# Differential attention on one Trainium2 core: the context queries' scores move into the free PSUM columns of two latent score runs

## The chip, the cores and the metric

The program runs on one core of a Trainium2 chip. Its engines work side by side, each through its own queue in order: TensorE (PE, matmuls into PSUM), VectorE (DVE), ScalarE (ACT), GpSimd (POOL), and SyncE (SP), which issues most of the DMA transfers. The metric is the device time of one execution in microseconds, as the median of several runs.

## What is computed

Two layers of a diffusion backbone over 512 latent tokens and 256 context tokens, model width 1024. Layer 0 is differential attention with 8 heads, each with two maps of head width 64; layer 1 is grouped-query attention. Layer 0 is what the change touches:

```python
k_all = jnp.concatenate([k, kc], axis=1)          # 512 latent + 256 context keys
v_all = jnp.concatenate([v, vc], axis=1)

def diff(qq, kk, vv, gate):
    o1 = sweep_attention(qq[..., 0, :], kk[..., 0, :], vv)
    o2 = sweep_attention(qq[..., 1, :], kk[..., 1, :], vv)
    o = o1 - lam.astype(o1.dtype) * o2
    o = rms_norm(o, subln_g) * (1.0 - lam_init)
    o = o.reshape(o.shape[0], o.shape[1], BRANCH_WIDTH)
    return (o * jax.nn.silu(gate)) @ w_out

y = diff(q, k_all, v_all, z)                      # latent queries read all 768 keys
yc = diff(qc, kc, vc, zc) if with_ctx_out else None   # context queries read 256 context keys
```

`sweep_attention` is a softmax over the keys for blocks of 128 queries. In between, the modulation (`adaln`) of both layers needs products of the conditioning vectors with large matrices (`ada_w`).

## The kernel before, in words

All matmuls keep about fp32 precision by splitting an operand into a high and a low fp32r part and adding three products (names with `hi`/`lo`, or `h`/`l` at the end). Weights stream in as `raw`, ScalarE casts them to `whi`, GpSimd subtracts to `wlo`.

PSUM has eight banks of 512 fp32 columns. Four are the single banks `bk` for projections, PV products and the like. Four are the two score tiles `sc`, each of two banks (`sc2()` hands them out in turn).

Layer 0's attention runs head by head. A head has four latent query tiles of 128 rows (qt 0 to 3) against 768 keys, and two context query tiles (qt 4 and 5) against the 256 context keys. For a latent tile, `unit` computes the scores of both maps: map m=0 in one score tile, m=1 in the other. As keys have width 64, the two maps use the upper and lower 64 rows of the array and are issued in pairs (`for m in (1, 0)`); three products (qh kh, qh kl, ql kh) for each half of 384 keys make 12 matmuls, chained so that nothing stands between them. For each map VectorE takes the maximum of 768 scores, ScalarE the exponential with its sum, VectorE the reciprocal; GpSimd scales map 0, and VectorE subtracts lambda times map 1 into the probabilities `pp`. Two query tiles share one `pp`, which `turn` transposes: on VectorE within blocks of 32, then by a store to DRAM (`dr`) and four gathers into `at`. `pv_steps` splits `at` into `ah` and `al` (ScalarE, VectorE) and multiplies with V.

For seven heads the context tiles have a unit of their own, `unit_ctx`: both tiles in one run of 12 matmuls of 256 columns, tile qt 4 in the first bank of each score tile and qt 5 in the second; one maximum over two groups of 256 columns per map, then exponentials, reciprocals of two columns, and a `turn` of width 128. The last head (h = 7) treats its context tiles in another way, which stays as it is in substance.

In the same stretch, `grp_mm` multiplies the modulation weights: twelve loads `araw` of 1 MB, one after the other through one tile (`bufs=1`), four matmuls of 32 output rows each. `grp_load` issues the next load when these matmuls have read the tile.

What sets the order: the whole program is recorded first, then `Plan` orders it. It prices each instruction (`price`), simulates the queues (`schedule`), with prices for DMA landing by size and for VectorE and GpSimd disturbing each other (`op.kind`), and finally shifts the priorities of single groups of instructions by random amounts that the numbers of the table `MOVES` fix. So a change of a price or of this table moves instructions on all engines, in both layers.

Of the kernel before, what the change touches and what calls it, by code (L numbers as in the profile page):

```python
# [16 lines left out]
P = 128  # L17
# [71 lines left out]
DRSPLIT = 1  # L89
DRB = 6  # L90
# [3 lines left out]
def f32(ap):  # L94
# [6 lines left out]
MOVES = (121443151, 661718012, 381041855, 51234840, 372779023, 957281565, 227970257, 105033711, 68446900, 773563299,  # L101
# [22 lines left out]
SLACK = 0  # L124


# [469 lines left out]
def tile_backbone(  # L596
# [692 lines left out]
    with pl.pool("t0") as t0:  # L1289
# [149 lines left out]
        def z_proj(h):  # L1439
# [12 lines left out]
            ws.release((h, 3))  # L1452
            szt[h] = sz
            gate_mul(h)

        def s_units(h, qts):
            res, pair = [], {}

# [922 lines left out]
```

## Time and profile before

| | us |
|---|---|
| median of 3 runs | 756.37 (755.59 to 760.27) |
| the profiled execution's own time | 757.93 |
| its span, first to last instruction | 755.8 |
| mean granted TensorE clock | 0.996 |

The profile comes from one execution. In its rows, times are in us from the start of the span, in groups the last figure of the busy column is the mean duration in ns; "idle before" is the time the engine stood still just before the group, and the name behind the arrow is what it waited for. A row of the timeline gives start, length, engine, operation, output and inputs, and a count of merged instructions. L509 is the line of a helper through which all instructions go. "MATMUL ... 64*128" is a matmul that uses 64 rows of the array, "128*32" one with 32 output rows. Matmuls overlap, so the price of one is read from start to start.

### The profile page before, as it was taken

The page shows a single profiled execution, that of the slowest core. Times are in us where ns is not written, and L with a number is a line of the kernel's source. Part 1 is how long each engine was busy: PE and PEld are TensorE (multiplying, and loading weights), DVE is VectorE, ACT ScalarE, POOL GpSimd, SP SyncE. Part 2 cuts the span into 40 slices and gives each one's busy share as a digit, 9 for nine tenths or more (in the row PEclk, how much of TensorE's full clock was granted, in tenths as well). Part 3 has the DMA queues.
Part 4 walks back from the last instruction along what each step waited for, and adds up shares of the span by engine and source line. Part 5 has one row for each costly group of instructions (what it writes and reads, how often), then busy time and mean ns, then how long its engine had stood idle before and what let it go on. Part 6 is the DMA issues. An engine that isn't in the chain of part 4 may idle for free. (4 is left out here: it accounts for less than half of the span.)

```text
span 755.8 us, 13984 instructions
## 1 busy us (share of the span) xinstructions
PE 733.9 (97%) x5046; PEld 654.3 (87%) x5046; DVE 567.1 (75%) x881; ACT 480.0 (64%) x1085; POOL 466.7 (62%) x512
## 2 busy tenths in 40 slices
PE   7999999999999999899999999999999989999996
PEld 6788888888878898797989998899999988888986
DVE  4445899988988869787889844789547787799744
ACT  6544477767676646666569853784476776678741
POOL 5463787885795738747755412467779887674201
PEclk9999999999999999999999999999999999999999
DMA  9933263647474655835666182034436785888613
GB/s 347 405 123 124 95 198 109 188 164 223 140 221 142 212 165 176 255 100 172 229 171 179 31 307 84 2 97 157 145 117 190 224 257 163 232 239 266 165 46 111
DMA packets 51444, 131.75 MB, mean 174 GB/s; under 512 B 6448, under 2 KB 27184, under 8 KB 49840
## 3 DMA queue, kind: packets, MB, share of 16 engines
q1 hardware_dynamic: 47952, 125.73, 52.7%
q10 hardware_dynamic: 3424, 5.15, 2.1%
q8 instruction: 39, 0.64, 0.4%
q14 instruction: 29, 0.24, 0.1%
HBM read 97.56 MB, written 29.10 MB: 168 GB/s over the span
## 5 line engine op out<-in xcount | busy, mean ns | idle before, releaser
L509 PE MATMUL bk<-whi,h 128*128 128x256 f32 (+1 forms) x1184 | 244.0, 298 | 2.9 <-DVE tb L509 1.8
L509 PE MATMUL bk<-h,whi 128*128 128x512 f32 (+2 forms) x832 | 222.4, 348 | 0.1
L509 POOL TENSOR_TENSOR wlo<-raw,whi 128x256 fp32r<-128x256 f32 x200 | 171.1, 879 | 56.1 <-ACT whi L509 53.7
L509 PEld LDWEIGHTS bk<-whi,h 128*128 128x128 f32 x1184 | 189.6, 189 | 13.9 <-issue 2.9
L509 PE MATMUL bk<-wlo,h 128*128 128x256 f32 (+1 forms) x592 | 172.3, 298 | 0.0
L509 PEld LDWEIGHTS bk<-h,whi 128*128 128x128 f32 x832 | 144.4, 188 | 15.6 <-issue 2.8
L509 PE MATMUL bk<-h,wlo 128*128 128x512 f32 (+2 forms) x416 | 144.0, 348 | 0.0
L509 POOL TENSOR_SCALAR pp<-pp,sm 128x768 f32<-128x768 f32 (+1 forms) x78 | 82.0, 1054 | 68.0 <-DVE sm L509 58.4
L509 PEld LDWEIGHTS bk<-wlo,h 128*128 128x128 f32 x592 | 109.8, 188 | 4.9 <-issue 1.6
L509 DVE TENSOR_REDUCE sm<-sc 128x1 f32<-128x768 f32 (+2 forms) x114 | 101.0, 893 | 14.7 <-PE sc L509 14.5
L509 DVE TENSOR_TENSOR al<-at,ah 128x512 fp32r<-128x512 f32 x103 | 98.7, 978 | 13.7 <-ACT ah L509 9.9
L509 ACT CAST whi<-raw 128x1024 fp32r<-128x1024 f32 (+1 forms) x70 | 71.5, 1023 | 27.1 <-PE bk L509 14.9
L509 PEld LDWEIGHTS bk<-h,wlo 128*128 128x128 f32 x416 | 78.3, 188 | 8.7 <-issue 2.4
L509 ACT CAST ah<-at 128x512 fp32r<-128x512 f32 x103 | 61.7, 618 | 33.3 <-PE bk L509 21.0
L509 DVE STREAM_TRANSPOSE pp<-pp 128x1536 f32<-128x1536 f32 (+1 forms) x39 | 61.4, 1577 | 5.7 <-POOL pp L509 5.6
L509 DVE SCALAR_TENSOR_TENSOR pp<-p,sm,pp 128x768 f32<-128x768 f32 (+1 forms) x46 | 55.8, 1219 | 4.4 <-POOL pp L509 2.8
L509 PE MATMUL sc<-qk,qk 64*128 64x384 f32 (+1 forms) x480 | 50.7, 341 | 0.4 <-DVE qk L509 0.4
L509 ACT ACTIVATE jk<-bk 128x128 f32<-128x128 f32 (+4 forms) x66 | 22.7, 345 | 41.8 <-PE bk L509 22.8
L509 ACT ACTIVATE pp<-sc,sm 128x768 f32<-128x768 f32 (+1 forms) x46 | 35.4, 770 | 21.5 <-DVE sm L509 20.8
L509 PEld LDWEIGHTS sc<-qk,qk 64*128 64x128 f32 x480 | 38.3, 184 | 10.7 <-issue 3.5
L509 POOL TENSOR_TENSOR sz<-sz,za 128x384 f32<-128x384 f32 (+1 forms) x24 | 28.3, 1180 | 23.8 <-ACT za L509 23.8
L509 ACT ACTIVATE za<-za 128x384 f32<-128x384 f32 (+1 forms) x72 | 40.0, 559 | 4.7 <-DVE za L509 4.1
(206 smaller groups left out, 1365.1 us busy)
## 6 DMA issues: line engine op xcount, KB each, us to landing
dr<-pp SPq DMA_DIRECT2D x32, 768.0 KB, 4.0
at<-dr SPq DMA_DIRECT2D x128, 192.0 KB, 4.3
raw<-in_a_w SPq DMA_DIRECT2D x30, 512.0 KB, 3.9
araw<-in_ada_g SPq DMA_DIRECT2D x12, 1024.0 KB, 7.0
raw<-in_b_w SPq DMA_DIRECT2D x20, 512.0 KB, 3.8
ag<-in_ada_s SPq DMA_DIRECT2D x16, 512.0 KB, 9.9
raw<-in_w_out SPq DMA_DIRECT2D x16, 512.0 KB, 4.5
sw<-qr ACTq DMA_DIRECT2D x32, 128.0 KB, 2.1
```

The source lines that it names most:

```text
L509: self.ops.append(getattr(eng, meth)(*args, **kw))
```

## The change

For heads 0 to 6 the separate context unit goes. The scores of context tile 4 are computed at the end of the run of latent tile 2, those of tile 5 at the end of the run of latent tile 3 (`CTX_AT`), into columns 768 to 1023 of the same score tiles, which the latent scores leave free. So that a matmul stays within one bank, the latent keys are cut into 512 and 256 columns instead of twice 384, in all heads. The two units then do their softmax for both the 768 and the 256 columns; reciprocals and the product with lambda work on two columns at once. The exponential of map 1 of the context rows goes into the tile (`at128`) that later takes the transposed result, where it had gone into a tile `p1`. A head's keys count as read (`s_end`) after its second pair of latent tiles. In the planner, the factor for single-input work on GpSimd goes from 0.25 to 0.6, the landing prices of transfers of 128 KB and 1 MB change, and `MOVES` is a new, shorter table.

```diff
+CTX_AT = {2: 0, 3: 1}
-MOVES = (121443151, 661718012, 381041855, 51234840, 372779023, 957281565, 227970257, 105033711, 68446900, 773563299,
...
+MOVES = (361629762, 413672696, 596582793, 497724196, 683463327, 110464215, 110999015, 165414765, 369530505, 1059228683,
...
-                op.kind = 0.75 if n <= 8 else 0.5 if sum(free_size(a) > 8 for a in ins) >= 2 else 0.25
+                op.kind = 0.75 if n <= 8 else 0.5 if sum(free_size(a) > 8 for a in ins) >= 2 else 0.6 if q == "POOL" else 0.25
...
-                rate, base = {196608: (207, 1450), 786432: (420, 900), 131072: (350, 2500)}.get(op.cost, (350, 1450))
+                rate, base = {196608: (207, 1450), 786432: (420, 900), 131072: (300, 1500), 1048576: (300, 2400)}.get(op.cost, (350, 1450))
...
-    def turn(pool, pp, w=384):
+    def turn(pool, pp, w=384, at=None):
...
-        at = pool.tile([P, 4, w], F32, tag=f"at{w}", name=nm("at"), bufs=ATB if w == 384 else 1)
+        if at is None:
+            at = pool.tile([P, 4, w], F32, tag=f"at{w}", name=nm("at"), bufs=ATB if w == 384 else 1)
...
+        def s_mm(sc, h, qt, lo, w, prev):
+            qh, ql, kh_, kl_ = qk[h]
+            tok = slice(qt * P, (qt + 1) * P)
+            for i, (a, b) in enumerate(((qh, kh_), (qh, kl_), (ql, kh_))):
+                for m in (1, 0):
+                    r = slice(m * 64, m * 64 + 64)
+                    o = flat_sc(sc[m])[:, lo:lo + w]
+                    if qt < NQ:
+                        b_ = b[r, lo:lo + w]
+                    else:
+                        o, b_ = by_a(o, 64), by_a(b[r, :], 192)[:, :, P:]
+                    with after(prev), chained(prev):
+                        prev = nc.tensor.matmul(o, a[r, tok], b_, start=i == 0, stop=i == 2)
+            return prev
...
             def unit(qt):
...
+                e = CTX_AT.get(qt) if h < KT - 1 else None
+                l = small(4)
+                sc = [sc2(), sc2()]
+                prev = s_mm(sc, h, qt, 0, 512, None)
+                prev = s_mm(sc, h, qt, 512, C, prev)
+                if e is not None:
+                    s_mm(sc, h, NQ + e, T, C, prev)
+                    if e == 0:
+                        ctx_tiles[h] = (
+                            t0.tile([P, 8, 2, 32], F32, tag="p0", name=nm("pp"), bufs=1),
+                            t0.tile([P, 4, P], F32, tag="at128", name=nm("at"), bufs=1))
+                    cp_, ct = ctx_tiles[h]
+                    cs = [unit_view(cp_, e), ct.rearrange("p a c -> p (a c)")[:, e * C:e * C + C].rearrange("p (b x) -> p b x", x=32)]
...
+                n = 1 if e is None else 2
+                for m in range(2):
+                    mx = small(2)
+                    for j in range(n):
+                        src = flat_sc(sc[m])[:, j * T:j * C + T]
+                        nc.vector.tensor_reduce(mx[:, j:j + 1], src, AX.X, ALU.max, negate=True)
+                        nc.scalar.activation(
+                            (cs if j else ps_)[m], src.rearrange("p (b x) -> p b x", x=32), AF.Exp, bias=mx[:, j:j + 1],
+                            accum_out=l[:, 2 * m + j:2 * m + j + 1])
+                    r = l[:, 2 * m:2 * m + n]
+                    nc.vector.reciprocal(r, r)
+                    if m == 1:
+                        nc.vector.tensor_tensor(r, r, nlam.to_broadcast([P, n]) if n > 1 else nlam, ALU.mult)
...
+                if qt % 2:
+                    res.append(turn(t0, pair[0]))
+                if e == 1:
+                    ctx_at[h].append(turn(t0, cp_, P, ct))
...
-            def unit_ctx():
...
-                for qt in (NQ, NQ + 1):
...
-                    nc.vector.tensor_reduce(mx, sc[m][:, :, :C], AX.X, ALU.max, negate=True)
...
-                if ch == 2:
+                if ch == (1 if h < KT - 1 else 2):
                     wrap(u[-1], None, lambda h=h: s_end(h))
```

How this moves instructions, at three places. First TensorE, at a context tile's scores. `sc_74` and `sc_75` are the two score tiles, the `qk` names are a head's qh, ql, kh, kl, and `h`/`whi` are activations and weights of a projection. Before, in head 1, the run of the context unit starts behind a projection's matmul:

```order
L509 MATMUL bk_70<-h_535,whi_1199 128x256
L509 MATMUL sc_75<-qk_1178,qk_1176 128x256
L509 MATMUL sc_74<-qk_1178,qk_1176 128x256
L509 MATMUL sc_75<-qk_1179,qk_1176 128x256
L509 MATMUL sc_74<-qk_1179,qk_1176 128x256
L509 MATMUL sc_75<-qk_1178,qk_1177 128x256
L509 MATMUL sc_74<-qk_1178,qk_1177 128x256
```

After, in head 3, the same forms follow the 512 columns of a latent tile:

```order
L501 MATMUL sc_75<-qk_2104,qk_2103 128x512
L501 MATMUL sc_74<-qk_2104,qk_2103 128x512
L501 MATMUL sc_75<-qk_2104,qk_2102 128x256
L501 MATMUL sc_74<-qk_2104,qk_2102 128x256
L501 MATMUL sc_75<-qk_2105,qk_2102 128x256
L501 MATMUL sc_74<-qk_2105,qk_2102 128x256
L501 MATMUL sc_75<-qk_2104,qk_2103 128x256
L501 MATMUL sc_74<-qk_2104,qk_2103 128x256
```

The six rows of 256 columns stand there twice in a row, first for the last latent keys, then for the context tile; then a projection goes on. In all, 41 score runs become 34, of which 14 have 18 matmuls.

Second, SP's queue around two loads of `araw` in head 3's stretch; `dr` is the store of transposed probabilities, `at` the gathers. Before:

```order
L509 DMA dr_2691<-pp_2600 128x1536
L509 DMA araw_2556<-in_ada_g 128x2048
L509 DMA at_2690<-dr_2691 32x4x384 x4
L509 DMA raw_2647<-in_a_w 128x1024
L509 DMA dr_2743<-pp_2726 128x512
L509 DMA araw_2702<-in_ada_g 128x2048
```

After:

```order
L501 DMA raw_2643<-in_a_w 128x1024
L501 DMA araw_2538<-in_ada_g 128x2048
L501 DMA araw_2725<-in_ada_g 128x2048
L501 DMA dr_2699<-pp_2590 128x1536
L501 DMA raw_2810<-in_a_w 128x1024
L501 DMA dr_2706<-pp_2588 128x512
```

The store and gathers that stood around and between the two loads now stand behind both. On TensorE the groups of matmuls that read these loads have 35 ordinary matmuls between them before, 38 wider ones and a score run after.

Third, TensorE in layer 1, where a query projection (`whi`, `wlo` with the tokens `h`) ends in a bank and the next one begins. Before:

```order
L509 MATMUL bk_72<-whi_7209,h_730_5258 128x256
L509 MATMUL bk_72<-wlo_7210,h_730_5258 128x256
L509 MATMUL bk_72<-whi_7209,h_731_5259 128x256
L509 MATMUL bk_72<-whi_7200,h_730_5258 128x256
L509 MATMUL bk_72<-wlo_7201,h_730_5258 128x256
L509 MATMUL bk_72<-whi_7200,h_731_5259 128x256
```

After, at the same projection:

```order
L501 MATMUL bk_71<-whi_7167,h_695_5216 128x256
L501 MATMUL bk_71<-wlo_7168,h_695_5216 128x256
L501 MATMUL bk_71<-whi_7167,h_696_5217 128x256
L501 MATMUL bk_73<-al_7516,vh 128x256 x2
L501 MATMUL bk_73<-ah_7568,vh 128x256 x2
L501 MATMUL bk_73<-ah_7568,vl 128x256 x2
L501 MATMUL bk_73<-al_7569,vh 128x256 x2
L501 MATMUL bk_73<-ident,q_6675 128x128
L501 MATMUL bk_73<-ident,q_6729 128x128
L501 MATMUL bk_73<-ident,q_6790 128x128
L501 MATMUL bk_73<-ident,q_6844 128x128
L501 MATMUL bk_71<-whi_7158,h_695_5216 128x256
```

PV products and transposes now stand between the two projections in that bank. On ScalarE, the squares for that query tile's norm (`jk`) stood behind the cast `qh` of the transposed query tile. Before:

```order
L509 CAST ah_7557<-at_7451 128x512
L509 CAST ah_7610<-at_7451 128x512
L509 COPY g_1125_7555<-bk_73 128x4x2x32
L509 CAST qh_7750<-bk_73 128x512
L509 ACTIVATE jk_7713,sm_7712<-bk_72 128x128
L509 ACTIVATE jk_7715,sm_7712<-bk_72 128x128
```

After:

```order
L501 CAST ah_7568<-at_7409 128x512
L501 CAST ac_7925<-gacc 128x512
L501 ACTIVATE jk_7671,sm_7670<-bk_71 128x128
L501 ACTIVATE jk_7673,sm_7670<-bk_71 128x128
L501 COPY g_1090_7513<-bk_73 128x4x2x32
L501 ACTIVATE sm_7720<-sm_7718,qrs_6672 128x1
```

They now stand ahead of the copy of the PV result (`g`), and the cast of the query tile comes some rows later.

More of the change, by code (lines that the diff above doesn't have):

```diff
@@ new lines, in unit @@
+                if qt % 2 == 0:
+                    pair[0] = t0.tile([P, 24, 2, 32], F32, tag="pp", name=nm("pp"), bufs=PPB)
+                ps_ = [unit_view(pair[0], qt % 2), t0.tile([P, T], F32, tag="p1", name=nm("p"), bufs=2).rearrange("p (b x) -> p b x", x=32)]
+                n = 1 if e is None else 2
[11 more added lines that the diff above has]
+                        nc.vector.tensor_tensor(r, r, nlam.to_broadcast([P, n]) if n > 1 else nlam, ALU.mult)
+                    for j in range(n):
+                        d, a = (cs if j else ps_)[0], (cs if j else ps_)[1]
+                        if m == 0:
+                            scaled(EP0, d, d, r[:, j:j + 1])
+                        else:
+                            nc.vector.scalar_tensor_tensor(d, a, r[:, j:j + 1], d, ALU.mult, ALU.add)
@@ new lines, in unit, with unit_last @@
+                if qt % 2:
+                    res.append(turn(t0, pair[0]))
+                if e == 1:
+                    ctx_at[h].append(turn(t0, cp_, P, ct))
+            def unit_last(qt):
+                if qt == NQ:
+                    sts["sc"] = sc2()
+                    pair[2] = t0.tile([P, 2, C], F32, tag="p0", name=nm("p"), bufs=1)
+                l = small(2)
+                qh, ql, kh_, kl_ = qk[h]
+                tok, prev, ps_ = slice(qt * P, (qt + 1) * P), None, []
+                sc = sts["sc"]
+                for i, (a, b) in enumerate(((qh, kh_), (qh, kl_), (ql, kh_))):
+                    for m in (1, 0):
+                        r = slice(m * 64, m * 64 + 64)
+                        with after(prev), chained(prev):
+                            prev = nc.tensor.matmul(k_a_j(sc[:, m, :C]), a[r, tok], by_k(b[r, :], 2), start=i == 0, stop=i == 2)
@@ L1509, in unit @@
-                    nc.scalar.activation(pv_, src, AF.Exp, bias=mx, accum_out=l[:, m:m + 1])
+                    nc.vector.tensor_reduce(mx, sc[:, m, :C], AX.X, ALU.max, negate=True)
+                    if m == 0:
+                        pt = pair[2][:, qt - NQ]
+                    else:
+                        pt = t0.tile([P, T], F32, tag="p1", name=nm("p"), bufs=2)[:, :C]
+                    nc.scalar.activation(pt, sc[:, m, :C], AF.Exp, bias=mx, accum_out=l[:, m:m + 1])
                     ps_.append(pt)
@@ L1558, in s_units @@
-            if qts[0] == NQ and h < KT - 1:
-                return res, [Step(unit_ctx, 1.0)]
-            sts = {}
-            cost = 1.2 if qts[0] < NQ else 0.5
-            return res, [Step(lambda qt=qt: unit(qt), cost) for qt in qts]
+                res.append(ps_[0])
+            if qts[0] == NQ:
+                if h < KT - 1:
+                    return ctx_at[h], []
+                sts = {}
+                return res, [Step(lambda qt=qt: unit_last(qt), 0.5) for qt in qts]
+            return res, [Step(lambda qt=qt: unit(qt), 1.6 if h < KT - 1 and qt in CTX_AT else 1.2) for qt in qts]
@@ L1731, in s_end @@
             try_split(h + 1)
-        w_o, subs = [], {}
+        w_o, subs, s_of = [], {}, []
         for h in range(KT):
```

89 lines of the change are left out of this document (8 added, 81 removed), and 35 rows, old and new, of the table MOVES.

## The prediction

> **What bounds the kernel now.** I read the page's first lines, then the table of stages, then the list of who made TensorE wait, then single places in the timeline.
>
> ```profile
> span 755.8 us, 13984 instructions
> PE 733.9 (97%) x5046; PEld 654.3 (87%) x5046; DVE 567.1 (75%) x881; ACT 480.0 (64%) x1085; POOL 466.7 (62%) x512
> ```
>
> TensorE is busy 97% of the span, and no other engine over 75%. The table of stages says where the remaining 22 us lie; its columns are the busy times of the five engines, the granted clock and the DMA share.
>
> ```profile
> core 0: us, PE busy (x) PEld busy (x) DVE busy (x) ACT busy (x) POOL busy (x), PEclk, DMA share, GB/s
> 0.00:20.00 20.00, 15.66 (x119) 12.34 (x123) 10.08 (x30) 12.14 (x23) 9.63 (x21) 1.00 0.92 350
> ...
> 72.00:422.00 350.00, 345.20 (x2403) 301.20 (x2402) 298.44 (x427) 232.91 (x495) 246.38 (x225) 1.00 0.56 173
> ...
> 600.00:700.00 100.00, 93.74 (x567) 84.78 (x566) 84.30 (x115) 75.65 (x166) 67.82 (x68) 0.98 0.80 233
> ...
> 748.00:756.00 8.00, 1.88 (x16) 1.68 (x15) 4.66 (x10) 0.97 (x4) 1.25 (x2) 0.79 0.55 197
> ```
>
> The attention of layer 0 (72 to 422 us) loses 4.8 us on TensorE, the second half of layer 1's attention (600 to 700) loses 6.3, start and end lose 4.3 and 6.1. So every instruction that TensorE no longer issues, and every wait that goes, shortens the end by as much. Two waits stand out:
>
> ```profile
> PE bk L509 <- DMA araw<-in_ada_g: 3.6, 2, 1.9
> ...
> PE bk L509 <- DVE tb L509: 1.8, 1, 1.8
> ```
>
> Two waits for the load of `araw` make 3.6 of the 4.8 us in layer 0; one wait for VectorE's `tb` makes 1.8 of the 6.3 in layer 1.
>
> **The change part by part.** *Fewer score runs.* A score matmul uses 64 rows of the array, two at a time; entering and leaving such a run has a price. Here is one separate context run of 12 matmuls between ordinary ones (start, length, count):
>
> ```profile
> 172.61 0.40 PE L509 MATMUL bk<-whi,h 128*128 128x256 f32 x2
> 172.85 0.28 PE L509 MATMUL bk<-wlo,h 128*128 128x256 f32 x1
> 173.06 0.97 PE L509 MATMUL sc<-qk,qk 64*128 64x256 f32 x12
> 173.96 0.50 PE L509 MATMUL bk<-whi,h 128*128 128x256 f32 x2
> 174.29 0.28 PE L509 MATMUL bk<-wlo,h 128*128 128x256 f32 x1
> ...
> 180.41 1.34 PE L509 MATMUL sc<-qk,qk 64*128 64x384 f32 x12
> 181.68 0.39 PE L509 MATMUL bk<-wlo,h 128*128 128x256 f32 x1
> ```
>
> Two ordinary 256-wide matmuls step 0.24 us, so 0.12 each. The one at 172.85 takes 0.21 until the run starts: 0.09 lost. The run takes 0.90, of which six pairs at 0.12 are 0.70: 0.20 lost. The two behind it take 0.33 instead of 0.24: 0.09 lost. So a run costs 0.38 us beyond its columns. Seven separate context runs become the tails of runs that exist anyway: 7 x 0.38 = 2.7 us off TensorE. The latent pieces go from 384+384 to 512+256 columns. A pair of 384 costs (1.27 - 0.20)/6 = 0.18, a pair of 256 0.12: cost goes with columns, and columns stay, so I take 0. Pairs of 512 are not in the trace; by columns they cost 0.23. Were that off by a tenth, the 96 pairs (32 units of 3) would move 2.2 us either way; that goes into the range.
>
> *The softmax of the context rows.* Per head VectorE did two reductions of 512 columns and now does four of 256; two reciprocals and one product with lambda fall away, since those of the latent rows now carry two columns.
>
> ```profile
> L509 DVE TENSOR_REDUCE sm<-sc 128x1 f32<-128x768 f32 x96 | 89.9, 945 | 12.7 <-PE sc L509 12.5
> L509 DVE TENSOR_REDUCE sm<-sc 128x2 f32<-128x512 f32 x14 | 9.4, 675 | 1.7 <-PE sc L509 1.6
> L509 DVE TENSOR_TENSOR sm<-sm,nlam 128x2 f32<-128x2 f32 x7 | 2.9, 413 | 0.1
> L509 DVE RECIPROCAL sm<-sm 128x2 f32<-128x2 f32 x14 | 2.0, 151 | 0.0
> L509 DVE TENSOR_REDUCE sm<-sc 128x1 f32<-128x256 f32 x4 | 1.7, 414 | 0.3 <-PE sc L509 0.3
> ```
>
> 28 x 0.414 = 11.6 comes, 9.4 + 2.9 + 2.0 = 14.3 goes: VectorE loses 2.7 us, all beside TensorE (it is busy 298 of 350 us there), so I count 0. Without that cover it would be a further gain. ScalarE's exponentials, GpSimd's scalings, the transposes and the DMAs keep their number and size. What changes is how long a unit holds the two score tiles: one more pair of reductions and exponentials.
>
> ```profile
> L509 ACT ACTIVATE pp<-sc,sm 128x768 f32<-128x768 f32 x32 | 28.8, 901 | 20.8 <-DVE sm L509 20.8
> L509 ACT ACTIVATE p<-sc,sm 128x256 f32<-128x256 f32 x18 | 8.5, 475 | 1.0 <-DVE sm L509 1.0
> L509 ACT ACTIVATION_READ_ACCUMULATOR pp<-sc,sm 128x1 f32 x46 | 9.0, 195 | 0.0
> ```
>
> The first reduction (0.95), two wide exponentials (2 x 1.10 with their readout) and two narrow ones (2 x 0.67) make 4.5 us until the next unit may write. In the new order the shortest stretch of TensorE work behind such a run is 24 matmuls of 512 and 7 of 256, which is 24 x 0.23 + 7 x 0.12 = 6.4 us (0.23 by the same columns). So this is covered by 1.9 us and counts 0. If ScalarE stands in other work, the next score run is late, and with it all behind it on TensorE.
>
> *The loads of `araw`.* One tile holds them, so load n+1 leaves when the matmuls of load n have read it.
>
> ```profile
> 225.60 1.07 PE L509 MATMUL bk<-araw,s 128*32 128x512 f32 x8 [1.70 <-DMA araw<-in_ada_g]
> ...
> 308.52 1.06 PE L509 MATMUL bk<-araw,s 128*32 128x512 f32 x8
> ...
> 319.78 1.07 PE L509 MATMUL bk<-araw,s 128*32 128x512 f32 x8 [1.91 <-DMA araw<-in_ada_g]
> ```
>
> The issue on SP between the latter two, and the view of the tile:
>
> ```profile
> 309.64 0.33 SPq L509 DMA_DIRECT2D araw<-in_ada_g  x1
> ```
>
> ```profile
> DMA to landing us min/median/max: 5.1/7.0/10.0
> ```
>
> The issue comes 1.1 us after the matmuls start (308.52 to 309.64), and landing takes 5.1 to 10.0, median 7.0. So 6.2 to 11.1 us of TensorE work must lie between two groups. In the order before, the second of these pairs has 36 matmuls of 256, 14 of 384 and 6 of 512 between: 4.3 + 2.5 + 1.4 = 8.2 at 0.12, 0.18 and 0.23; the trace shows 319.78 - 1.91 - 308.52 = 9.35, so a group and its switches add 1.15. Three groups are close in the new order: 38 matmuls of 384 and a score run of 12 (6.8 + 1.4); 38 of 256, 7 of 384 and a run of 18 (5.9 + 1.8); 37 of 256, 3 of 384 and two runs of 12 (5.0 + 2.8). With 1.15 each that is 9.3, 8.8 and 8.9, which after the 1.1 until the issue covers a landing of 8.2, 7.7 and 7.8. The median is covered, the maximum is not: between 0 and 1.8 + 2.3 + 2.2 = 6.3 us of waiting. If the slower half of the loads spreads evenly from 7.0 to 10.0, these cost 0.5, 0.9 and 0.8 on average, and half of that over all loads: 1.1. In the first of them SP issues nothing between the two loads, so no gather takes its bandwidth. The two old waits go: -3.6 + 1.1 = -2.5. SP is blocked there until the second group has run, and the transposed probabilities queued behind it leave later by some us; their PV matmuls stand two or more score units on, so I count 0.
>
> *The turn of one bank in layer 1.* A query projection ends at 629.72, and the next group writes the same bank at once, so TensorE waits for the norms on ScalarE and the rotation on VectorE:
>
> ```profile
> 629.72 0.28 PE L509 MATMUL bk<-whi,h 128*128 128x256 f32 x1
> 631.80 0.36 PE L509 MATMUL bk<-whi,h 128*128 128x256 f32 x1 [1.80 <-DVE tb L509]
> ...
> 633.43 0.63 PE L509 MATMUL bk<-ah,vl 128*128 128x256 f32 x2
> ...
> 636.53 0.33 PE L509 MATMUL bk<-whi,h 128*128 128x256 f32 x1
> ```
>
> Single stretches of TensorE in the table of stages (busy time, granted clock, DMA share, GB/s) show the clock behind this gap and behind the two of the loads:
>
> ```profile
> 226.00:230.00 4.00, 4.00 (x32) 1.00 1.02 340
> ...
> 320.00:324.00 4.00, 4.00 (x32) 1.00 0.58 179
> ...
> 634.00:636.00 2.00, 2.00 (x10) 0.50 0.99 249
> ```
>
> In the new order eight matmuls and four transposes stand between the end of that group and the next writer, at least 8 x 0.12 = 0.9 us, and ScalarE takes the norms before, not behind, the cast of the query tile. The wait can vanish or stay whole (0 to 1.8); I take 0.6, so -1.2. From 633.43 to 636.53 thirteen matmuls (ten of 256, three of 384) take 3.1 us that are 10 x 0.12 + 3 x 0.18 = 1.7 at full speed: the granted clock was 0.50 there. I count these 1.4 with the wait.
>
> [...]
>
> *The rest.* The new table moves rows everywhere, and layer 1 does not change otherwise. The other waits of 600 to 700 are 6.3 - 1.8 = 4.5 us. They could all go (-4.5) or double (+4.5); I take 0, as the work and its banks are the same.
>
> *Sum.* -2.7 (runs) -2.5 (`araw`) -1.2 and -1.4 (bank turn and clock) = -7.8. The profiled execution took 757.93, so 750.1. It lies 1.56 above the median of 756.37, about the price of the slow clock; if that was its accident, the median gives 756.37 - 6.4 = 750.0. I say 750.0.
>
> **The rivals.** *Waits grow back.* TensorE runs shorter, but VectorE and ScalarE come in as late as before, so only the score runs count: 757.93 - 2.7 = 755.2. For it: VectorE is busy 85% in layer 0. Against it: it waits there too, and itself loses 2.7.
>
> [...]
>
> *Layer 1's other waits go as well*: 750.0 - 4.5 = 745.5. For it: they come from places, not from throughput. Against it: nothing in the diff aims at them.
>
> *Slower: the context gather holds the score tiles.* The narrow exponential of head h+1 now writes the tile in which the context rows of head h came back, so it must wait until that gather has landed and been split. ScalarE takes it in order, the score tile stays full, and TensorE stops at the next score run. Behind the third unit of heads 1 to 6 TensorE has 9.9, 8.5, 13.9, 9.1, 24.0 and 7.1 us of work (counted as above); less 4.5 that leaves 5.4, 4.0, 9.4, 4.6, 19.5 and 2.6. If the gather, now queued with the large one, comes 7.5 us later than that allows, 2.1 + 3.5 + 2.9 + 4.9 = 13.4 us of waits arise: 763.4. From a lateness of about 6 us it eats the gain. Against it: ScalarE has room (busy 233 of 350 us), and it would need such lateness in several heads.
>
> **How the numbers follow.** Forecast 0.45 (746.5 to 753.5 by itself); clock 0.12; waits grow back 0.18; layer 1 better still 0.17; slower rival 0.08. One per cent of the median, about what a measurement of this kernel can tell from no change, is 7.6 us: 748.8 and 763.9. Below 748.8 lie nearly all of the layer-1 case and a third of the forecast: 0.32. Above 763.9 lies half of the slower rival: 0.04. Within: 0.64. The range 743.5 to 758.0 reaches 2 us beyond the layer-1 case and 3 beyond the grown waits, and leaves out the slower rival and some of the ends, about 0.16.
>
> **What would show it.** Score runs of 18 matmuls with the same 0.38 of loss; TensorE's wait for `araw` near 1 us; its wait for `tb` under 1 us and the clock at 1.00 in 600 to 700; fewer reciprocals on VectorE. Wrong would be: TensorE waiting at `sc` for ScalarE in layer 0, `araw` waits of 3 us or more, or a stage 600 to 700 that loses more than 6 us.

## The result and the profile after

| | before | after |
|---|---|---|
| median, us | 755.59 (754.11 to 760.27, 7 runs) | 749.61 (745.36 to 757.76, 7 runs) |
| the profiled execution, us | 757.93 | 751.56 |
| its span, us | 755.8 | 749.8 |
| ratio of the times | | 0.9908 (95% interval 0.988 to 0.9936) |

The forecast of 750.0 us lies 0.4 us from the median. The change makes the kernel faster by 0.6 to 1.2%, about the 1% that the prediction set as the least that can be told from no change. The run of 757.76 us had a granted clock of 0.990 and counts as slow, and the ratio leaves it out. The profile's first lines and its table of stages, after the change:

```profile
span 749.8 us, 13955 instructions
PE 731.8 (98%) x5046; PEld 651.8 (87%) x5046; DVE 552.5 (74%) x874; ACT 482.0 (64%) x1085; POOL 464.4 (62%) x512
```

```profile
0.00:20.00 20.00, 14.44 (x112) 11.52 (x112) 10.57 (x30) 11.72 (x23) 8.70 (x19) 1.00 0.93 356
72.00:422.00 350.00, 347.23 (x2424) 304.09 (x2421) 289.48 (x425) 235.12 (x498) 251.67 (x228) 1.00 0.58 173
...
600.00:700.00 100.00, 96.68 (x608) 87.45 (x607) 83.94 (x121) 77.81 (x169) 63.16 (x65) 1.00 0.80 235
...
338.00:340.00 2.00, 2.00 (x13) 1.78 (x13) 1.73 (x5) 2.00 (x6) 0.00 (x0) 0.61 0.65 238
340.00:342.00 2.00, 2.00 (x16) 1.70 (x16) 0.45 (x1) 1.14 (x2) 0.78 (x2) 0.54 0.80 328
```

Layer 0 loses 2.8 us on TensorE (4.8 before), 600 to 700 loses 3.3 (6.3), the start 5.6 (4.3). The granted clock (third figure from the end) is 1.00 throughout 600 to 700, but 0.61 and 0.54 in four microseconds of layer 0: (0.39 + 0.46) x 2 = 1.7 us are lost there. So the stretch of slow clock is not gone; it stands elsewhere.

The list of who made TensorE wait, and the view of the tile `araw`:

```profile
PE bk L501 <- ACT ah L501: 3.7, 4, 2.3
...
PE bk L501 <- DVE al L501: 1.2, 2, 1.0
```

```profile
DMA to landing us min/median/max: 4.7/5.2/7.6
```

Neither `araw` nor `tb` is among those waited for. A new wait of 2.3 us has come, for ScalarE's cast `ah`. In the timeline of TensorE one joined run, the new wait, and the place where `tb` had been waited for:

```profile
207.12 0.28 PE L501 MATMUL bk<-h,wlo 128*128 128x256 f32 x1
207.34 1.68 PE L501 MATMUL sc<-qk,qk 64*128 64x512 f32 x18
208.94 0.50 PE L501 MATMUL bk<-h,whi 128*128 128x256 f32 x2
209.28 0.28 PE L501 MATMUL bk<-h,wlo 128*128 128x256 f32 x1
...
337.57 0.50 PE L501 MATMUL bk<-ah,vhi 128*128 128x256 f32 x2 [2.26 <-ACT ah L501]
...
627.05 0.50 PE L501 MATMUL bk<-al,vh 128*128 128x256 f32 x2 [1.00 <-DVE al L501]
628.01 0.66 PE L501 MATMUL bk<-ident,q 128*128 128x128 f32 x4 [0.46 <-ACT g L501]
```

The joined run steps 1.60 us (207.34 to 208.94): three pairs each of 512 and 256 columns for the latent tile and three pairs of 256 for the context tile. The 0.10 lost ahead of it (0.22 instead of 0.12) and the 0.10 behind it (0.34 instead of 0.24) are those of a separate run before, within 0.01.

**A balance that the experiments use.** From the timeline of one execution I take the end of the last matmul, all idle times in brackets, and 1.7 us for each stretch of slow clock; the rest is the work that TensorE had to do. Two executions of one kernel differ in this rest by up to 1.4 us.

| kernel | last matmul ends | waits | slow clock | rest |
|---|---|---|---|---|
| before | 749.9 | 15.4 | 1.7 | 732.8 |
| before, a second profile | 747.9 | 12.9 | 1.7 | 733.3 |
| after | 743.8 | 11.4 | 1.7 | 730.7 |
| after, a second profile | 741.1 | 9.1 | 0 | 732.1 |

### The profile page after: what moved, and what is told of

It is laid out like the page before. It is cut to its first block, busy times and chain, and to the rows that moved or that the text cites. A ratio compares the mean times of both kernels' runs of the same rounds, so it can differ in the third digit from the quotient of the medians.

```text
span 749.8 us, 13955 instructions
## 1 busy us (share of the span) xinstructions
PE 731.8 (98%) x5046; PEld 651.8 (87%) x5046; DVE 552.5 (74%) x874; ACT 482.0 (64%) x1085; POOL 464.4 (62%) x512
## 4 chain that ended last, share of the span: by engine, by line
PE 79%; DMA 9%; DVE 5%; ACT 2%; POOL 2%; issue 2%; SPq 0%; ACTq 0%; DVEq 0%; POOLq 0%
PE bk L501 65%; PE sc L501 14%; DMA at<-dr 3%; DMA dr<-pp 2%; DMA raw<-in_a_w 2%; DVE pp L501 1%; DVE al L501 1%; DMA ag<-in_ada_s 1%; ACT ah L501 1%; DMA xt<-in_x 1%; DMA sw<-qr 0%; POOL pp L501 0%; SPq L501 0%; POOL qr L501 0%; DVE sm L501 0%
## 5 line engine op out<-in xcount | busy, mean ns | idle before, releaser
L501 PE MATMUL bk<-h,whi 128*128 128x512 f32 (+2 forms) x832 | 224.8, 350 | 0.0
L501 DVE TENSOR_REDUCE sm<-sc 128x1 f32<-128x768 f32 (+1 forms) x128 | 102.7, 811 | 19.0 <-PE sc L501 13.9
L501 DVE TENSOR_TENSOR al<-at,ah 128x512 fp32r<-128x512 f32 x103 | 93.6, 929 | 22.5 <-ACT ah L501 17.4
L501 POOL TENSOR_SCALAR pp<-pp,sm 128x768 f32<-128x768 f32 (+1 forms) x78 | 79.1, 1017 | 43.1 <-DVE sm L501 42.5
L501 POOL TENSOR_TENSOR sz<-sz,za 128x384 f32<-128x384 f32 (+1 forms) x24 | 31.0, 1299 | 39.7 <-ACT za L501 38.5
L501 PE MATMUL sc<-qk,qk 64*128 64x256 f32 (+1 forms) x480 | 49.5, 343 | 0.0
L501 DVE SCALAR_TENSOR_TENSOR pp<-p,sm,pp 128x768 f32<-128x768 f32 x32 | 42.0, 1314 | 3.0 <-POOL pp L501 1.6
```

The lines of the kernel that those rows point to most:

```text
L501: self.ops.append(getattr(eng, meth)(*args, **kw))
```

## Experiments

Most of the kernels take the planned order and move a few rows on one engine. A small function added behind the plan takes rows [a, b) of an engine's order and sets them ahead of row `to`; all other rows keep their order. Each edit below is the list of such moves. Times are medians, and ratios are to runs of the kernel before on the same chip.

**1. Undoing the joining alone.**

```diff
-        em.chain(pl.plan())
+        em.chain(moved_order(pl, pl.plan(), MOVED))
+MOVED = [('PE', 486, 492, 495), ('PE', 535, 541, 544),
...
+    ('PE', 2207, 2213, 2216), ('PE', 2271, 2277, 2280)]
```

> The changed kernel, in which on TensorE alone the six context matmuls of each of the fourteen joined runs stand three ordinary matmuls behind the twelve latent ones, so that each is a run of 64-row matmuls by itself again; every other row keeps its place. My theory (a run by itself costs 0.38 us of TensorE, 0.09 at its entry, 0.20 inside and 0.09 at its exit): fourteen more runs cost 14 x 0.38 = 5.3 us, so 749.6 becomes about 755, the share that TensorE is busy in 72 to 422 rises from 347.2 to about 352 of a layer that is longer by as much, and its rows show the same 0.38 in each split place. Rival (the runs were hidden by other engines or by waits, and the gain of the change came from elsewhere): 749 to 751, with longer runs but shorter waits.

Measured: 754.44 us, ratio to before 0.9978 (0.9964 to 0.9991), beside 0.9908 for the change itself: 0.0070 x 755.6 = 5.3 us given back, as forecast (3.9 against the second measurement of the change, in run 9; each of these ratios has an interval of 0.1 to 0.3% either way). One of the fourteen places in the timeline of TensorE:

```profile
210.58 1.32 PE L501 MATMUL sc<-qk,qk 64*128 64x512 f32 x12
211.83 0.50 PE L501 MATMUL bk<-h,whi 128*128 128x256 f32 x2
212.17 0.28 PE L501 MATMUL bk<-h,wlo 128*128 128x256 f32 x1
212.38 0.62 PE L501 MATMUL sc<-qk,qk 64*128 64x256 f32 x6
212.93 0.50 PE L501 MATMUL bk<-h,whi 128*128 128x256 f32 x2
213.27 0.28 PE L501 MATMUL bk<-h,wlo 128*128 128x256 f32 x1
```

The run of six steps 0.55 (212.38 to 212.93), and its three pairs are worth 3 x 0.12 = 0.35: 0.20 lost inside. The matmul ahead of it takes 0.21 instead of 0.12, the two behind it 0.34 instead of 0.24. That is 0.39 for a run, 5.5 for fourteen. The balance says 6.3 (rest 737.1 against a mean of 730.8 for six profiles with joined runs), which its scatter allows. The share that TensorE is busy in 72 to 422 did not rise to 352, as I had written: it cannot exceed the 350 us of the window. The layer became longer: the last score run of layer 0 ends at 405.0 instead of 400.0. The rival falls: nothing hid the runs.

**2. Taking the two `araw` waits out of the kernel before.**

```diff
+MOVED = [('PE', 1423, 1427, 1447), ('PE', 2054, 2058, 2075)]
```

> The kernel before, in which on TensorE alone the two groups of gather matmuls that wait for a landing in layer 0 (3.6 us of waits together) stand about 2.4 us of other matmuls later. My theory: the two waits shrink to 1.2 or less and nothing takes their place, so the time falls by 2.4 to 3.6 us, 755.6 to about 752.5. Rival (the wait grows back behind another late landing, or the groups behind them, which use their rows, are late instead): the waits of TensorE in 72 to 422 still sum to about 4.8 and the time is 754.5 to 756.

Measured: 755.23 us, ratio 0.999 (0.9974 to 1.0005): no gain. In the timeline of TensorE, and of ScalarE below it, at the first of the two places:

```profile
227.38 1.07 PE L509 MATMUL bk<-araw,s 128*32 128x512 f32 x8
...
232.94 1.32 PE L509 MATMUL sc<-qk,qk 64*128 64x384 f32 x12 [0.80 <-ACT p L509]
```

```profile
229.92 0.62 ACT L509 CAST ah<-at 128x512 fp32r<-128x512 f32 x1 [3.13 <-DMA at<-dr]
230.45 0.90 ACT L509 ACTIVATE pp<-sc,sm 128x768 f32<-128x768 f32 x1
...
231.89 0.90 ACT L509 ACTIVATE p<-sc,sm 128x768 f32<-128x768 f32 x1 [0.46 <-DVE sm L509]
```

The group no longer waits (it waited 1.70 before). But ScalarE stands 3.13 us for a gather (2.89 at this place in the kernel before); the two exponentials that empty the score tiles are queued behind that cast, and TensorE now reaches the next score run 0.80 too early. In the kernel before, where it waited for `araw`, this wait did not show. Behind the second group stands a wait of 1.41 for `al`. The stretch from the first to the last score run of layer 0 is 332.9 us long, against 333.3 and 331.8 in the two profiles of before. The rival holds: the waits grew back.

**3. Breaking up the wait of 1.80 in the kernel before.** The transposes of q and the next gathered group fill the gap on TensorE; ScalarE makes the norms and that group's cast first.

```diff
+MOVED = [('PE', 4224, 4228, 4215), ('PE', 4206, 4210, 4215), ('ACT', 761, 763, 760), ('ACT', 765, 766, 762)]
```

> The kernel before, at the one wait of 1.80 us at 631.8: the four transposes of q stand behind the last five matmuls into the bank that is waited for, the four matmuls of the next gathered group stand ahead of the matmuls that wait, and ScalarE makes the sums of squares and that group's cast ahead of the q copy. My theory: the wait of 1.80 breaks into pieces of under 1 us that sum to about 1.0, and the stretch at a granted clock of 0.50 that followed it (1.4 us) is gone: 600 to 700 loses about 4 instead of 6.3, the time falls by about 2.2, 755.6 to 753.4. First rival (the stretch of slow clock has another cause than the gap): only the 0.8 of the wait go, 754.8, and the clock is 0.50 again within 634 to 637. Second rival (ScalarE's next exponential is late by the moved cast, and TensorE waits at the score banks): no gain, 755.6, with a wait at sc of 0.5 to 1.

Measured: 755.68 us, ratio 0.9995 (0.9975 to 1.0015): no gain. That is the time of the second rival, and its wait at the score banks is there (0.39), but the larger part is another. TensorE, and ScalarE's cast:

```profile
629.58 0.51 PE L509 MATMUL bk<-ah,vh 128*128 128x256 f32 x2 [1.56 <-ACT ah L509]
...
631.43 0.44 PE L509 MATMUL sc<-kh,qh 128*128 128x384 f32 x1 [0.39 <-ACT pp L509]
```

```profile
628.91 0.62 ACT L509 CAST ah<-at 128x512 fp32r<-128x512 f32 x1 [0.52 <-DMA at<-dr]
```

The group that I put into the gap was itself late: its gather landed only at 628.9. So 1.56 + 0.39 = 1.95 us of waits stand where 1.80 stood. No slow clock followed in this execution (the granted clock is 1.00 from 630 to 636); what that means is seen in the next one and at the end.

**4. The kernel before, a second profile.**

> The kernel before, word for word, for a second profile of it. If its waits belong to the kernel: 3.6 us at the two gather groups, 1.80 at 631.8 and the granted clock of 0.50 at 634 to 636 stand in it again, each within 0.3 us. If the stretch of slow clock is an accident of one execution, the wait of 1.80 is there and the clock behind it is 1.00, or the stretch is at another place.

Measured: 755.93 us in the one run. The timeline of TensorE, and one stretch of the table of stages:

```profile
225.97 1.06 PE L509 MATMUL bk<-araw,s 128*32 128x512 f32 x8 [2.00 <-DMA araw<-in_ada_g]
...
630.33 0.36 PE L509 MATMUL bk<-whi,h 128*128 128x256 f32 x1 [1.80 <-DVE tb L509]
```

```profile
632.00:634.00 2.00, 2.00 (x9) 2.00 (x9) 0.91 (x2) 0.87 (x2) 1.60 (x1) 0.50 0.97 223
```

The waits at 226 and 630 belong to the kernel, and here the clock of 0.50 came behind the second again. The second `araw` wait, of 1.91 at 320, does not: it is missing here, and in run 3 as well. It hung on one load that took 10.0 us to land; the longest took 8.0 here. So about half of the 3.6 us that the prediction wanted to save belonged to the one profiled execution.

**5. Turns of order in the changed kernel, at its new wait (TensorE and ScalarE) and at 627 (VectorE).**

```diff
+MOVED = [('PE', 2183, 2187, 2213), ('ACT', 387, 388, 385), ('DVE', 743, 744, 742)]
```

> The changed kernel with three small turns of order: at the new wait of 2.26 us at 337.6 the matmuls of the late gathered group stand on TensorE behind the next score run, and ScalarE makes that run's exponential ahead of the late group's cast; in layer 1 VectorE makes the low part al ahead of a block transpose at the wait of 0.50 at 627. My theory: what waits there is ScalarE's queue behind one late gather, so the wait of 2.26 shrinks to under 1.0 and no other takes its place; layer 1 gains 0.3 more: 749.6 becomes about 747.5, and about 746 if the stretch of slow clock behind the wait goes with it. Rival (the gathers are late as a whole, and a wait that is taken away comes back at the next group, as it did where the two araw groups were moved): a wait of 1 to 2.5 at another gathered group or at a score bank within 30 us, and 749 to 750.

The "wait of 0.50 at 627" of the text is a misreading: 0.50 is the length of that row, and its wait is 1.00. Measured: 752.41 us, ratio 0.9944 (0.992 to 0.9968): no better than the change itself, and by the medians rather worse. In layer 0 the wait of 2.26 fell to 0.83, as forecast. In layer 1 the turn did harm:

```profile
622.73 0.50 PE L501 MATMUL bk<-al,vh 128*128 128x256 f32 x2 [0.46 <-DVE al L501]
623.69 0.66 PE L501 MATMUL bk<-ident,q 128*128 128x128 f32 x4 [0.46 <-ACT g L501]
625.98 0.38 PE L501 MATMUL bk<-whi,h 128*128 128x256 f32 x1 [1.64 <-DVE tb L501]
```

`al` comes earlier, but VectorE still has the transpose to do ahead of `tb`, so TensorE only reaches the next result of VectorE sooner and waits 1.64 there. The rival is right about the kind of thing, at another place than it named. The profiled execution, 748.66 us, is the fastest of the twelve: it shows 1.1 us more of waits at this place than the changed kernel has (2.56 against 1.46), but not what the rest of the median's 2.8 us consists of.

**6. Two transfers moved behind four gathers, SyncE alone.**

```diff
+MOVED = [('SP', 150, 152, 156)]
```

> The changed kernel, with SyncE alone changed: the two loads (768 KB and 256 KB of table and weights, issued at 323.4 and 324.5) that stand ahead of the four gathers whose group TensorE waits for at 337.6 stand behind those four. My theory (the gathers land late because the two loads and eight gathers share the queues in one burst): they land in about 4.5 us rather than 7.1, and the wait of 2.26 falls below 1; 749.6 becomes about 748. Rival (the gathers are late since they are issued late, when their table rows have been written): they land as late as before and the wait stays within 0.4 of 2.26, the time at 749 to 750; or the two loads are late instead and a wait of 1 or more stands at whi or raw.

The text names the two transfers wrongly: they are a store of probabilities to DRAM (`dr`, 256 KB) and a load of weights (`raw`, 512 KB). SyncE's issues, after the change and here:

```profile
323.43 0.92 SPq L501 DMA_DIRECT2D dr<-pp  x2
324.45 1.13 SPq L501 DMA_DIRECT2D raw<-in_a_w  x1
326.76 5.34 SPq L501 DMA_DIRECT2D at<-dr  x8
```

```profile
323.00 0.33 SPq L501 DMA_DIRECT2D dr<-pp  x1
326.32 1.75 SPq L501 DMA_DIRECT2D at<-dr  x4
328.17 0.38 SPq L501 DMA_DIRECT2D dr<-pp  x1
328.65 0.36 SPq L501 DMA_DIRECT2D raw<-in_a_w  x1
```

Measured: 746.89 us, ratio 0.9891 (0.9846 to 0.9936), from four runs. The four gathers among the DMA issues of 318 to 345 us, after the change and here (KB each, median us to landing):

```profile
at<-dr SPq DMA_DIRECT2D x4, 192.0 KB, 7.1
```

```profile
at<-dr SPq DMA_DIRECT2D x4, 192.0 KB, 4.3
```

```profile
72.00:422.00 350.00, 348.88 (x2457) 306.87 (x2454) 291.47 (x428) 238.92 (x506) 252.04 (x228) 1.00 0.57 175
```

They land in 4.3 us instead of 7.1, the wait at `ah` is gone, and layer 0 loses 1.1 us instead of 2.8. The first of them leaves at almost the same time, 326.3 against 326.8, so the rival of a late issue falls. The new wait came from the order of transfers: in the changed kernel two stores, a load and eight gathers left SyncE within 9 us.

**7 and 8. The planner without its table of moves: the kernel before, and the joined runs with the old prices.**

```diff
-MOVES = (
...
+MOVES = ()
```

> The kernel before without its table of moves, so that the planner alone sets the order. No theory gives its time, which I put at 758 to 775; it is the base of the next run, and shows what the table is worth. TensorE's time outside its waits and outside slow clock should be that of the kernel before, 733.3 within 1, if the waits alone are what the table changes.

> The joined runs alone: the changed kernel's code with the planner's old prices and without a table of moves, to stand beside the run before it. My theory (joining is worth 0.38 us for each of seven runs of context scores, all of it in TensorE's time outside waits): TensorE's time outside waits is 2.7 us less than in the run before it, within 0.7, and the difference of the two times is that plus what the waits do by chance of the order, which can be several us of either sign. Rival (the gain of the change lies in its order and prices): TensorE's time outside waits is the same within 0.7.

Measured: 763.18 us (ratio 1.0087, 1.0047 to 1.0126) and 758.13 us (1.0037, 1.0016 to 1.0058), 5.05 apart. In the balance the last matmul ends 3.4 earlier: waits 15.9 and 13.8, slow clock 3.4 each, rest 736.1 and 734.8. The rest falls by 1.3, which lies between the forecast of 2.7 and the rival's 0, outside the 0.7 of both and within the scatter; this pair alone doesn't decide it, run 1 does. My expectation that the rest of the plain kernel before is that of the tuned one was wrong by 2.8: the table moves TensorE's time outside its waits as well, and by what is not shown. Both keep the waits of 1.8 in layer 1 for `al` and `tb`. The wait for `araw` (2.00 in the first) is missing in the second: in these two profiles it goes with the joined runs, without any table, though one profile each cannot tell that from the scatter of a landing.

**9 to 11. The changed kernel again, the turn of SyncE again, and that turn with VectorE's transpose in layer 1 behind `al`, a maximum and the rotation.**

```diff
+MOVED = [('SP', 150, 152, 156), ('DVE', 742, 743, 748)]
```

> The changed kernel, word for word, beside the next two on one chip. If its waits belong to the kernel: the wait of 2.26 us at ScalarE's cast of the gathered group stands again at 335 to 343, within 0.4, and 600 to 700 loses 2.8 to 3.8. The slow stretch of the clock, which in every profile so far lasts 3.4 us and costs 1.7, need not stand behind it: I expect one or none of them, at a place where one wait fills more than 1.6 us. Time 747.5 to 751.5.

> The kernel with the two transfers of SyncE behind the four gathers, once more, for the difference to the changed kernel on the same chip. My theory (the burst of transfers made the gathers late): 2.0 to 3.5 us faster than the run before it, and no wait over 1 us in layer 0. Rival (the gain seen was the scatter of single executions): within 1 us of it.

> The run before, and in layer 1 VectorE makes the block transpose behind al, the score maximum and the rotation (ta, tb) instead of ahead of them, where TensorE waited 1.14 for al. My theory: that wait falls under 0.4, tb is not late (it was, when al alone went ahead), and the time is 0.7 to 1.2 us below the run before it. Rival (VectorE bounds this stretch, so a wait that goes comes back behind another of its results): waits of TensorE for VectorE in 610 to 640 sum to 1.1 or more again, and the time is the same.

Measured on one chip: 750.26 us (ratio 0.9927, 0.9898 to 0.9955), 748.50 (0.9915, 0.9884 to 0.9946) and 748.26 (0.9906, 0.9875 to 0.9936). The new wait of the changed kernel is there again, but shorter than my bound, and no slow clock follows it (1.00 from 330 to 350):

```profile
336.81 0.51 PE L501 MATMUL bk<-ah,vhi 128*128 128x256 f32 x2 [1.38 <-ACT ah L501]
```

With the turn of SyncE the four gathers land in 4.1 us (median) instead of 6.3, the last matmul ends at 739.4 instead of 741.1, and the wait at `ah` is gone a second time; though a wait of 1.10 at 270 for `arow`, 0.38 in run 11, broke my bound of 1. The time is 1.8 us lower, a little under the 2.0 that I forecast, and the intervals overlap: the cause of the new wait is shown by the landing times of two pairs of runs, its price is not yet shown by the measured times. In run 11 the waits for VectorE in 610 to 640 are 0.73 and 0.85, both for `al`, 1.6 in all: as its rival says, the wait moved. Nothing is gained there that the runs can tell.

**12. The joined runs with the new prices, without the table.**

> The changed kernel with its new prices and without its table of moves, to stand beside the joined runs with the old prices (758.1). If the new prices took layer 1's waits away, the waits of 1.76, 1.80 and 0.80 us there are gone here too and the time is 750 to 753; if the table did, they stand here as there, and the time is 756 to 760.

Measured: 759.70 us (ratio 1.0051, 1.0029 to 1.0073), no better than run 8. Each reading has half of it right. The list of waits:

```profile
PE bk L488 <- POOL sqs L488: 1.7, 1, 1.7
PE bk L488 <- DVE al L488: 1.6, 2, 1.5
PE bk L488 <- DVE kn L488: 1.3, 1, 1.3
```

The long waits of layer 1 (1.76, 1.80 and 0.80 in run 8) are gone with the new prices, but others have come: 1.7 for `sqs` and 1.5 for `al` in layer 0, 1.3 for `kn` in 422 to 600. So the new prices move the waits, and the table of moves, drawn up for these prices, takes many of them out: 759.7 - 750.3 = 9.4 us against run 9, on the same chip. In the balance the last matmul ends 10.0 us later than in run 9: 4.8 of this are waits, 1.7 slow clock, and 3.5 lie in the rest, for a reason that is not shown.

The ratios to before split the gain another way. Taking the old table out gives 1.0087 (run 7), joining then 1.0037 (run 8), the new prices 1.0051 (run 12), and the new table 0.9927 (run 9). With intervals of up to 0.4% either way, joining is worth 0.5%, the new prices by themselves nothing that the intervals can tell, and the new table 1.2% where the old one was worth 0.9%.

## Why the prediction was right, step by step

**Fewer score runs, -2.7: right.** The rest in the balance is 733.3 on average over four profiles with the order of before (runs 2, 3, 4 and the first one) and 730.8 over six of the changed kernel and its turns (two of it, and runs 5, 6, 10 and 11): -2.5, with single profiles up to 1.4 from their mean. As the tables alone move the rest by more than that (2.8 in run 7), the balance can't give these 2.5 to the joining; run 1 can, which leaves the order of all else alone: a separate run still costs 0.39 there, and seven make 2.7. The step from 384 + 384 to 512 + 256 columns was counted at 0 with 2.2 either way; a latent run of 12 steps 1.27 in the prediction's row and 1.25 us in run 1's, so it was 0 within 0.02 a run.

**The loads of `araw`, -2.5: the step was wrong in both halves, and half of the size came.** The waits went from 3.6 to 0, not to 1.1. The landing was taken at its median of 7.0 and maximum of 10.0 of that one execution; in the changed order it is 5.2 and 7.6. So the new landings were over-priced, and a wait elsewhere was put at nothing. What replaced them is not a late `araw` but a late gather: -3.6 + 2.3, so -1.3 in the profiled executions. And 1.9 of the 3.6 belonged to that one execution (run 4). The prediction counted that the DMAs "keep their number and size"; that a joined unit sends its latent and its context stores and gathers off together (the two `dr` and eight `at` of run 6) stands in its slower rival as a danger for the score tiles, not in the sum. "Waits grow back", a rival at 0.18, has this half: in run 2 TensorE, coming sooner, met ScalarE behind a late gather, and in the changed kernel it did so at another gather, late by the order of SyncE's queue (runs 6 and 10). The layer's busy share says -2.0 for the whole stage.

**The turn of one bank, -1.2: right in kind, other waits took most of its place.** `tb` is no longer waited for (1.80 to 0), but 1.00 for `al` and 0.46 for `g` now stand at 627 to 628. Runs 3, 5 and 11 each tried to take this place apart, and each time 2.0 to 2.6 us of waits stood there again.

**The clock, -1.4: wrong.** The stretch costs 1.7, not 1.4, and it came back in layer 0. The chance of 0.12 given to the clock stands for this case, 750.0 + 1.4 = 751.4; the profiled execution took 751.56. Whether a stretch comes differs between executions of one kernel (of the two profiles of the changed kernel one has a stretch of 1.7 and the other none), so it should have been in the range, not in the sum.

**Layer 1's other waits, 0 with 4.5 either way: the sum missed 1.6.** In 551 to 690 all waits fell from 5.6 to 2.2 (5.1 to 2.7 in the second profiles). Of these, 1.8 were `tb`; the other 1.6 are what is left of 3.1 that went, less the 1.5 that came at 627 to 628. They belong to the rival of 745.5, about a third of what it claimed. The wait of 1.23 at 655.9 for `ah` and one of 0.56 for an exponential are gone. Run 12 beside run 8 has lower waits in this stage under the new prices and higher ones in others; how much of the 1.6 is theirs and how much the table's was not separated.

**VectorE's softmax and the holding of the score tiles, both 0: right.** TensorE never waits for a score tile between the first and the last score run of layer 0, and VectorE's groups show the work as planned, 32 narrow maxima (28 more than before), and products and reciprocals of two columns; its busy time fell from 567.1 to 552.5:

```profile
L501 DVE TENSOR_REDUCE sm<-sc 128x1 f32<-128x256 f32 x32 | 13.1, 414 | 5.3 <-ACT pp L501 3.2 <-ACT whi L501 0.8 <-ACT p L501 0.7
...
L501 DVE TENSOR_TENSOR sm<-sm,nlam 128x2 f32<-128x2 f32 x14 | 7.3, 525 | 0.3
...
L501 DVE RECIPROCAL sm<-sm 128x2 f32<-128x2 f32 x28 | 4.4, 161 | 7.1 <-ACT at L501 6.0 <-ACT pp L501 0.8
```

So the -7.8 against the profiled execution came out at -6.4: in the balance -2.1 of work, 0 of clock, and -4.0 of waits (start +1.3, layer 0 -2.0, layer 1 -3.4, the rest +0.1); the other 0.3 lies outside the stretch up to the last matmul. That the median was met within 0.4 us is in part luck, as errors met: 1.4 of clock that did not go and 1.3 that the start lost more (0.2 in the second profiles), against some 2 us of waits in layer 1 that the sum had not counted. What the change is named for is worth 2.7 of some 6 us by the rows of run 1; the rest came with the new order, and of its waits only the one at `ah` was traced to its cause.

## What to carry to other kernels

Price a switch of the array's form by three numbers read from start to start (the matmul ahead, the run, the matmuls behind) and multiply: of all terms here, this one held best (0.38 us a run in the rows of before, 0.39 in run 1). A wait on a queue in order is a place where several late things meet; before counting it as gain, look at what ScalarE, VectorE and the DMA queue are doing at that moment, because in runs 2, 3, 5 and 11 TensorE only met the next of them (waits of 0.80, 1.56, 1.64 and 0.85 us). And a wait or a slow stretch that one profile shows may be that execution's own: of three profiles in which the `araw` groups stand where they did before, one had the second wait of 1.91, and of four in the order of before, two had the slow clock of 1.7 us.

## What the runs showed that I had not expected

**The slow clock comes in pieces of one size, on a fixed grid, and is a lottery.** Every stretch found inside the span of TensorE's work (nine, in seven profiles) lost 1.7 us at a granted clock of 0.50. The first and the last tenth of a microsecond of the one in the kernel before, in the table of stages:

```profile
633.20:633.30 0.10, 0.10 (x3) 0.10 (x2) 0.10 (x1) 0.10 (x1) 0.10 (x1) 0.60 0.00 0
...
636.60:636.70 0.10, 0.10 (x3) 0.10 (x2) 0.10 (x2) 0.00 (x0) 0.10 (x1) 0.83 1.14 261
```

It begins at 633.30 - 2 x 0.40 x 0.1 = 633.22 and ends at 636.60 + 2 x 0.17 x 0.1 = 636.63, so it lasts 3.41 us; the eight that were read in such slices (before, after, runs 4, 6, 7 and 8) last 3.412 to 3.414. Two profiles had two each. The two microseconds in which each of them begins, run 8 and then run 7, in the table of stages:

```profile
18.00:20.00 2.00, 1.73 (x6) 1.48 (x7) 1.12 (x3) 1.52 (x3) 1.65 (x3) 0.74 1.02 406
...
622.00:624.00 2.00, 1.35 (x8) 1.35 (x9) 1.86 (x5) 0.63 (x2) 0.15 (x1) 0.78 1.02 403
```

```profile
18.00:20.00 2.00, 1.74 (x5) 1.55 (x6) 1.12 (x3) 1.51 (x3) 1.65 (x3) 0.50 1.01 404
...
228.00:230.00 2.00, 1.15 (x8) 0.16 (x8) 1.45 (x2) 0.89 (x2) 2.00 (x2) 0.91 1.09 232
```

In run 8 the first stretch begins at 20 - 2 x 0.26 x 2 = 18.96, the second at 624 - 2 x 0.22 x 2 = 623.12: 604.16 apart, which is 177.0 times 3.413. In run 7 they begin at 18.0 and 230 - 2 x 0.09 x 2 = 229.64: 62.0 times. So the stretches of one execution begin on a grid of 3.413 us; a step of this grid is called a period here.

A wait of TensorE stands ahead of most stretches, but its length alone does not settle whether one comes. Those at 633.22 (before), 631.16 (run 4), 338.45 (after), 229.6 (run 7) and 218.6 (run 12) each followed a period in which one whole wait lay, of 1.80, 1.80, 2.26, 2.00 and 1.72 us. The other two away from the start, in runs 6 and 8, came 0.95 and 0.46 us after TensorE last stood still (until 623.11 and 622.65). The wait of 1.70 at 225.6 in the kernel before also lay wholly in one period (its stretch at 633.22 fixes the grid) and was followed by none, and its wait of 1.91 at 319.8 was cut by a boundary into 1.32 and 0.59 and was followed by none. The clock also falls behind the last matmul, and that start marks the grid too: it lies at 752.69 in the kernel before, 35.0 periods behind the stretch at 633.22, and at 748.04 after the change, 120.0 periods behind the one at 338.45. With this run 5, which has no inner stretch, can be read as well: the fall lies at 743.23, so its wait of 1.64 at 626.0 lay wholly in one period, and none followed. In run 4 a boundary at 224.98 cut the wait of 2.00 into 1.01 and 0.99, and in the changed kernel one period held the waits of 1.00 and 0.46 at 627 to 628; neither was followed by a stretch. So a limit would have to lie between 1.70 and 1.72 us of waits in a period, on one wait each, which is too little to show one. Nor is it explained why the two stretches near 18 us came; that of run 7 followed a period with 0.64 us of waits.

**The scatter between executions goes with it.** Of 70 further executions of the kernel before, ten had a mean granted clock of 0.998 or more and a median of 754.3 us; 43 had 0.995 to 0.997 and 755.5; twelve had 0.992 to 0.994 and 757.4; five had less and 760.5. One stretch lowers the mean by 1.71 / 756 = 0.0023. That the slow clock makes all of this difference is not shown; longer waits in an execution may bring both.
